# ScalarE copies both halves of an accumulator to a row, and VectorE adds the halves from that row

## The chip, the cores and the metric

The kernel runs on one core of a Trainium2 chip. The metric is the device time of one execution in microseconds (us), as the median of several runs. A profile is the hardware profiler's record of one further execution.

Five engines appear. PE is TensorE, and its record is split into matmuls (PE) and weight loads (PEld). DVE is VectorE, ACT is ScalarE, POOL is GpSimd, and SP is SyncE, which issues most of the DMAs. Each engine works through its own queue in order, and semaphores tie the queues together.

## The reference

One block of a hybrid network, on one sequence of 256 tokens with a model width of 2048, all in float32:

```python
z = h @ w_in                       # h: normalized x; all projections of the mixer at once
(dq, dkk, dv, dz, db, da, gq, gk, gv, glow, gr, su, gates) = split_columns(z, IN_SIZES)
qkv = silu(causal_depthwise_conv(concatenate([dq, dkk, dv]), dn_conv_w))
...                                # gated delta rule (DeltaNet), gated with silu(dz)
...                                # gated linear attention (GLA) from gq, gk, gv, glow, gr
...                                # S5 state space model over su, a scan over the 256 tokens
...                                # gates mix the three, then w_mix_out
...                                # cross-attention over 256 memory rows
...                                # FFN: two projections, a causal convolution over 3 tokens,
...                                # gelu of the one times the other, then the output projection
```

Widths of the projections: dq, dk, dv and dz 1024 each, gq and gk 512, gv, gr and su 1024, gates 3 x 2048; the FFN has 5632 hidden units, twice.

## The kernel before, in words

Every large matrix product is made in three partial products, so that the fast float32r format of TensorE gives nearly float32. The weights come by DMA as `raw` (SyncE, L205), 128 x 1024 at a time, which is two k-tiles of 128 rows by 512 columns. ScalarE casts them to their high part `whi` (L206) and VectorE subtracts to get the low part `wlo` (L206 too, since both stand in one line). There are four buffers of raw and three each of the high and the low part. The activations are held as a high and a low half beside each other, 2 x 256 columns.

`mm3` (L209 to L221) multiplies one 128 x 128 block: the high part of the weights with both halves at once, 512 columns, into all of an accumulator (L218, or L221 for the last k-tile), and the low part with the high half, 256 columns, into the first half of the accumulator (L219). So one accumulator is a PSUM bank of 128 x 512 whose two halves have to be added in the end. There are five such banks for accumulators ("acc") and three for other work ("mx").

`total` (L223) does that addition, and it is the function that changes. `proj` (L229) goes through one slab of 512 output columns: four accumulators, eight groups of weights for 16 k-tiles, and in the end the slab's `evac` for each of the four accumulators in turn. The evac functions call `total` and go on with the sum:

- `su_evac` (L1085, for the S5 input): total, then a product with `rx`, the inverse norm (L1090). rx comes out of work that waits for the whole of x (L992, L996).
- `conv_silu` (L382, for dq, dk and dv): total, an activation that scales it (L387), three steps of the convolution on VectorE (L389), Tanh (L392), a product (L393).
- the gated evac of dz and gr (L627 ff.), and those of keys and queries (L1183, L1184, L1335, L1343), some of which give `out`, the place for the sum.
- the FFN's evac (L1441 to L1458): total, a product with the inverse norm (L1444), and for every other accumulator the convolution (L1448, L1450) and the gelu (L1452); then the product of both (L1456) and its split in two parts (L305, L306).

152 totals are made in the program. `row()` gives a row of 128 x 256 from the pool `t1`, `row2()` one of 128 x 512 from the same pool; the evacuation of the gates (L1154) and the GLA's low-rank input use `row2` already.

The order of the instructions on each engine is not written out by hand: a scheduler with a model of the machine's times sets it when the program is built. `load_w` (L203) runs with a raised priority. Besides the projections there are background generators, which are fed in at set rates between the groups of weights: the set-up and the 255 steps of the S5 scan (VectorE, L932 to L934), the core of DeltaNet (L519, L702 to L722) and that of GLA. A change in what stands in a pool or an engine thus moves instructions elsewhere too.

Of the kernel before, what the change touches and what calls it, by code (L numbers as in the profile page):

```python
# [9 lines left out]
F32 = mybir.dt.float32  # L10
# [8 lines left out]
P = 128  # L19
T = 256  # L20
# [3 lines left out]
NW = 512  # L24
# [64 lines left out]
class Net:  # L89
# [131 lines left out]
            nc.tensor.matmul(acc, hi, both, start=start, stop=True)  # L221

    def total(self, acc, out=None):  # L223
        r = self.row() if out is None else out
        self.nc.scalar.copy(r, acc[:, T:2 * T])  # L225
        self.nc.vector.tensor_add(r, r, acc[:, 0:T])  # L226
        return r

    def proj(self, w, KT, rhs, evac, n=NW, wide=True):  # L229
# [81 lines left out]
    def open_main(self):  # L311
        c = self.ctx
        self.main_stack = ExitStack()
        self.sp = self.main_stack.enter_context(self.pool("sp"))
        self.s16 = self.main_stack.enter_context(self.pool("s16", bufs=1))
        self.s8 = self.main_stack.enter_context(self.pool("s8", bufs=3))
        self.s4 = self.main_stack.enter_context(self.pool("s4", bufs=6))
        self.t1 = self.main_stack.enter_context(self.pool("t1", bufs=8))
        self.jv = self.sp.tile([P, P], F32, name="jv")
        self.ja = self.sp.tile([P, T], F32, name="ja")  # L320

# [10 lines left out]
        return self.t1.tile([P, T], F32, name="r1", tag="r1")  # L332

    def row2(self):
        return self.t1.tile([P, NW], F32, name="r2", tag="r2", bufs=2)

    def small_cols(self, small, ab_in):
        nc = self.nc
# [1235 lines left out]
```

## Time and profile before

| what | value |
|---|---|
| runs shown | 1943.83, 1946.19 and 1947.27 us |
| their median | 1946.19 us |
| the profiled execution's own time | 1940.68 us |
| its span | 1938.9 us |
| mean granted clock of TensorE in it | 0.993 |
| bytes moved by DMA | 363.93 MB, 188 GB/s in the mean |

The span goes from the first to the last instruction of the profile; the time of the execution lies 1.8 us around it. In the rows below, a group's row reads: line of the code, engine, operation, output and inputs by their names in the program, form, count, then its busy time in us, the mean of one instruction in ns, and the idle time of the engine ahead of it with what ended that. A row of waits reads: engine and tile that waited, the arrow, the engine, tile and line waited for, then us in all, how often, and the longest. A row of a timeline starts with the instruction's start and its duration, and the bracket at its end is the idle time ahead of it and what ended it. A row of a stretch gives its bounds, its length and the busy time of PE, PEld, DVE, ACT and POOL, then the granted clock as a share of full speed, the DMAs' busy share and GB/s.

### The profile page before, as it was taken

The page shows a single profiled execution, that of the slowest core. Times are in us where ns is not written, and L with a number is a line of the kernel's source. Part 1 is how long each engine was busy: PE and PEld are TensorE (multiplying, and loading weights), DVE is VectorE, ACT ScalarE, POOL GpSimd, SP SyncE. Part 2 cuts the span into 40 slices and gives each one's busy share as a digit, 9 for nine tenths or more (in the row PEclk, how much of TensorE's full clock was granted, in tenths as well). Part 3 has the DMA queues.
Part 4 walks back from the last instruction along what each step waited for, and adds up shares of the span by engine and source line. Part 5 has one row for each costly group of instructions (what it writes and reads, how often), then busy time and mean ns, then how long its engine had stood idle before and what let it go on. Part 6 is the DMA issues. An engine that isn't in the chain of part 4 may idle for free.

```text
span 1938.9 us, 28177 instructions
## 1 busy us (share of the span) xinstructions
PE 1878.7 (97%) x10440; PEld 1565.4 (81%) x10440; DVE 1419.8 (73%) x2719; ACT 951.8 (49%) x1426; POOL 67.4 (3%) x117
## 2 busy tenths in 40 slices
PE   7989899999999999999999997999999999999997
PEld 6778788777778688878877986888888888888886
DVE  6878999996579999967666756766666666644445
ACT  5655544343565444444455655555555555534442
POOL 0000012020000000000000000000000000000000
PEclk9999999999999999999999998999999999999999
DMA  7535477684445576666576544655666555676664
GB/s 254 174 109 172 152 206 233 191 254 131 131 121 172 184 219 179 213 218 203 186 264 210 173 155 144 213 184 174 190 195 189 187 185 185 206 224 200 200 192 135
DMA packets 107482, 363.93 MB, mean 188 GB/s; under 512 B 12320, under 2 KB 20896, under 8 KB 106832
## 3 DMA queue, kind: packets, MB, share of 16 engines
q1 hardware_dynamic: 97696, 328.32, 54.9%
q0 software_dynamic: 9648, 33.81, 5.3%
q8 instruction: 82, 1.34, 0.3%
q14 instruction: 56, 0.46, 0.1%
HBM read 350.47 MB, written 11.61 MB: 187 GB/s over the span
## 4 chain that ended last, share of the span: by engine, by line
PE 86%; DVE 6%; issue 4%; DMA 2%; ACT 1%; POOL 0%; SPq 0%; DVEq 0%; ACTq 0%; POOLq 0%
PE acc L218 25%; PE acc L219 14%; PE acc L287 13%; PE acc L285 13%; PE acc L286 13%; DVE wlo L206 2%; PE acc L221 2%; PE mx L922 2%; DMA raw<-in 1%; DVE f L519 1%; DVE mm L932 0%; PE mx L183 0%; PE mx L947 0%; PE mx L641 0%; ACT whi L206 0%
## 5 line engine op out<-in xcount | busy, mean ns | idle before, releaser
L206 DVE TENSOR_TENSOR wlo<-raw,whi 128x1024 fp32r<-128x1024 f32 (+1 forms) x632 | 753.0, 1195 | 417.2 <-ACT whi L206 415.1
L206 ACT CAST whi<-raw 128x1024 fp32r<-128x1024 f32 (+1 forms) x632 | 646.7, 1029 | 724.8 <-PE acc L286 376.0
L218 PE MATMUL acc<-aa,whi 128*128 128x512 f32 x2085 | 725.8, 401 | 11.5 <-DVE r L226 9.7
L219 PE MATMUL acc<-aa,wlo 128*128 128x256 f32 x2224 | 555.2, 284 | 9.9 <-DVE wlo L206 9.9
L219 PEld LDWEIGHTS acc<-aa,wlo 128*128 128x128 f32 x2224 | 421.9, 190 | 53.3 <-DVE wlo L206 20.9
L218 PEld LDWEIGHTS acc<-aa,whi 128*128 128x128 f32 x2085 | 386.1, 190 | 82.2 <-issue 11.7
L285 PE MATMUL acc<-whi,aa 128*128 128x512 f32 (+1 forms) x704 | 269.8, 384 | 0.0
L286 PE MATMUL acc<-whi,aa 128*128 128x512 f32 (+1 forms) x704 | 268.4, 382 | 0.0
L287 PE MATMUL acc<-wlo,aa 128*128 128x512 f32 (+1 forms) x704 | 253.3, 385 | 3.7 <-DVE wlo L206 3.7
L287 PEld LDWEIGHTS acc<-wlo,aa 128*128 128x128 f32 x704 | 131.9, 188 | 33.6 <-DVE wlo L206 7.3
L286 PEld LDWEIGHTS acc<-whi,aa 128*128 128x128 f32 x704 | 132.4, 188 | 26.4 <-issue 1.1
L285 PEld LDWEIGHTS acc<-whi,aa 128*128 128x128 f32 x704 | 132.3, 188 | 26.2 <-issue 1.2
L285 PE MATMUL acc<-whi,ach 128*128 128x512 f32 x352 | 136.9, 389 | 0.0
L286 PE MATMUL acc<-whi,acl 128*128 128x512 f32 x352 | 136.9, 389 | 0.0
L287 PE MATMUL acc<-wlo,ach 128*128 128x512 f32 x352 | 123.4, 389 | 0.0
L932 DVE TENSOR_TENSOR mm<-M,X 128x128 f32<-128x128 f32 x254 | 98.6, 388 | 5.3 <-ACT X L926 0.6
L286 PEld LDWEIGHTS acc<-whi,acl 128*128 128x128 f32 x352 | 66.0, 188 | 13.8
L287 PEld LDWEIGHTS acc<-wlo,ach 128*128 128x128 f32 x352 | 66.1, 188 | 13.7
L285 PEld LDWEIGHTS acc<-whi,ach 128*128 128x128 f32 x352 | 66.1, 188 | 13.7
L934 DVE TENSOR_TENSOR X<-X,s__868 128x64 f32<-128x64 f32 x255 | 71.5, 280 | 4.5
L933 DVE TENSOR_TENSOR s__868<-mm 128x64 f32<-128x64 f32 x255 | 56.5, 222 | 4.7
L226 DVE TENSOR_TENSOR r<-r,acc 128x256 f32<-128x256 f32 x143 | 57.1, 414 | 0.4 <-ACT r L225 0.3
(454 smaller groups left out, 1865.6 us busy)
## 6 DMA issues: line engine op xcount, KB each, us to landing
raw<-in SPq DMA_DIRECT2D x600, 512.0 KB, 4.1
raw<-in SPq DMA_DIRECT2D x32, 256.0 KB, 2.7
gd<-r POOLq DMA_DIRECT2D x24, 256.0 KB, 4.7
f<-gd POOLq DMA_DIRECT2D x12, 512.0 KB, 5.3
f<-Rd POOLq DMA_DIRECT2D x4, 512.0 KB, 7.0
f<-in POOLq DMA_DIRECT2D x4, 512.0 KB, 4.0
gp<-in POOLq DMA_DIRECT2D x8, 256.0 KB, 4.5
xn<-in POOLq DMA_DIRECT2D x1, 2048.0 KB, 11.1
```

The costliest lines, as they stand in the source:

```text
L206: self.last = (nc.scalar.copy(hi, raw), self.seq(lambda: nc.vector.tensor_sub(lo, raw, hi.bitcast(F32))))
L218: nc.tensor.matmul(acc, hi, both, start=start, stop=False)
L219: nc.tensor.matmul(acc[:, :T], lo, x[:, 0, :], start=False, stop=False)
L221: nc.tensor.matmul(acc, hi, both, start=start, stop=True)
L226: self.nc.vector.tensor_add(r, r, acc[:, 0:T])
L285: nc.tensor.matmul(accs[t], xh[:, ts_], hi[:, kk, :], start=(kt == 0), stop=False)
L286: nc.tensor.matmul(accs[t], xl[:, ts_], hi[:, kk, :], start=False, stop=False)
L287: last[:] = [nc.tensor.matmul(accs[t], xh[:, ts_], lo[:, kk, :], start=False, stop=(kt == KT - 1))]
L922: nc.tensor.matmul(ps[:, n, c, :], self.Bl[c][rs, ft, :], su[rs, ft, tk], start=True, stop=True, tile_position=(32 * q, 0))
L932: nc.vector.tensor_mul(m, self.M, prev[:, None].broadcast_to([P, 2, 2, 32]))
L933: nc.vector.tensor_add(s, m[:, :, 0, :], m[:, :, 1, :])
L934: nc.vector.tensor_add(X[:, :, :, t], X[:, :, :, t], s)
```

## The change

`total` copies the whole accumulator, both halves, into a row of 128 x 512 from `row2`; VectorE then adds the two halves of that row, into its first half or into `out`. The pool `t1` loses two of its eight rows of 128 x 256, and the ring of `row2` has three rows instead of two. A sum without `out` lives in its row of the ring until its last reader is done.

```diff
     def total(self, acc, out=None):
-        r = self.row() if out is None else out
-        self.nc.scalar.copy(r, acc[:, T:2 * T])
-        self.nc.vector.tensor_add(r, r, acc[:, 0:T])
+        both = self.row2()
+        self.nc.scalar.copy(both, acc)
+        r = both[:, :T] if out is None else out
+        self.nc.vector.tensor_add(r, both[:, :T], both[:, T:])
         return r
...
-        self.t1 = self.main_stack.enter_context(self.pool("t1", bufs=8))
+        self.t1 = self.main_stack.enter_context(self.pool("t1", bufs=6))
...
     def row2(self):
-        return self.t1.tile([P, NW], F32, name="r2", tag="r2", bufs=2)
+        return self.t1.tile([P, NW], F32, name="r2", tag="r2", bufs=3)
```

Line numbers behind L225 are one higher after the change; the copy is L225 in both, the add L226 before and L227 after. The orders that follow were read from the built programs; a row is a line, an operation, and output and inputs, with a number on a tile's name where it tells one from another.

The first place is ScalarE's queue at the end of the dk projection, where `r_1054` and the like are the sums of the accumulators. Before:

```order
L206 CAST whi<-raw 128x1024 x3
L225 COPY r_1054<-acc 128x256
L206 CAST whi<-raw 128x1024
L387 ACTIVATE r_1057<-r_1054,cwh 128x256
L392 ACT_TABLE_LOAD
L392 ACTIVATE r_1062<-r_1057 128x256
L225 COPY r_1065<-acc 128x256
L387 ACTIVATE r_1068<-r_1065,cwh 128x256
L392 ACTIVATE r_1073<-r_1068 128x256
L225 COPY r_1086<-acc 128x256
L387 ACTIVATE r_1089<-r_1086,cwh 128x256
L206 CAST whi<-raw 128x1024 x5
```

After:

```order
L455 ACT_TABLE_LOAD
L455 ACTIVATE eg<-eg 128x16
L206 CAST whi<-raw 128x1024 x5
L225 COPY r_1054<-acc 128x512
L225 COPY r_1065<-acc 128x512
L225 COPY r_1086<-acc 128x512
L206 CAST whi<-raw 128x1024
L388 ACTIVATE r_1057<-r_1054,cwh 128x256
L206 CAST whi<-raw 128x1024
L393 ACTIVATE r_1062<-r_1057 128x256
L388 ACTIVATE r_1068<-r_1065,cwh 128x256
L225 COPY r_1097<-acc 128x512
```

Three copies now stand in a row, with five casts ahead of them, and the scalings (L387, now L388) and the Tanh (L392, now L393) stand behind; before, each copy stood behind the scaling of the accumulator ahead of it.

The second place is VectorE's queue at the same end of dk; `f_829` and `bl_450` belong to the set-up of the S5 scan, and `L893` (L894 after) is the first that reads what a DMA brings for it. Before:

```order
L206 TENSOR_TENSOR wlo<-raw,whi 128x1024
L389 SCALAR_TENSOR_TENSOR r_1057<-r_1054,cwh,r_1057 128x255
L389 SCALAR_TENSOR_TENSOR r_1057<-r_1054,cwh,r_1057 128x254
L389 SCALAR_TENSOR_TENSOR r_1057<-r_1054,cwh,r_1057 128x253
L393 SCALAR_TENSOR_TENSOR f_837<-r_1062,r_1057 128x4x64
L226 TENSOR_TENSOR r_1065<-r_1065,acc 128x256
L389 SCALAR_TENSOR_TENSOR r_1068<-r_1065,cwh,r_1068 128x255
L389 SCALAR_TENSOR_TENSOR r_1068<-r_1065,cwh,r_1068 128x254
L389 SCALAR_TENSOR_TENSOR r_1068<-r_1065,cwh,r_1068 128x253
L393 SCALAR_TENSOR_TENSOR f_837<-r_1073,r_1068 128x4x64
L226 TENSOR_TENSOR r_1086<-r_1086,acc 128x256
L893 TENSOR_TENSOR f_829<-f_824,bl_450 128x1024
```

After:

```order
L227 TENSOR_TENSOR r_1054<-r_1054 128x256
L227 TENSOR_TENSOR r_1065<-r_1065 128x256
L227 TENSOR_TENSOR r_1086<-r_1086 128x256
L206 TENSOR_TENSOR wlo<-raw,whi 128x1024
L390 SCALAR_TENSOR_TENSOR r_1057<-r_1054,cwh,r_1057 128x255
L390 SCALAR_TENSOR_TENSOR r_1057<-r_1054,cwh,r_1057 128x254
L390 SCALAR_TENSOR_TENSOR r_1057<-r_1054,cwh,r_1057 128x253
L206 TENSOR_TENSOR wlo<-raw,whi 128x1024
L394 SCALAR_TENSOR_TENSOR f_837<-r_1062,r_1057 128x4x64
L390 SCALAR_TENSOR_TENSOR r_1068<-r_1065,cwh,r_1068 128x255
L227 TENSOR_TENSOR r_1097<-r_1097 128x256
L894 TENSOR_TENSOR f_829<-f_824,bl_450 128x1024
```

The three adds now stand together and ahead of the convolution, and two subtractions of the weights (L206) stand between them and L894, where before the convolutions of two accumulators stood ahead of L893 and the next subtraction behind it.

The third place is ScalarE's queue at the end of su; `r_368` to `r_380` are the four sums, `rxr` the row of the inverse norm, `aa` the normalized activations. Before:

```order
L206 CAST whi<-raw 128x1024 x3
L225 COPY r_368<-acc 128x256
L225 COPY r_372<-acc 128x256
L225 COPY r_376<-acc 128x256
L206 CAST whi<-raw 128x1024
L225 COPY r_380<-acc 128x256
L206 CAST whi<-raw 128x1024 x2
L996 COPY rxr<-mx 128x256
L206 CAST whi<-raw 128x1024
L308 ACTIVATE aa<-f_102,vec 128x256 x4
```

After:

```order
L206 CAST whi<-raw 128x1024 x3
L225 COPY r_368<-acc 128x512
L225 COPY r_372<-acc 128x512
L225 COPY r_376<-acc 128x512
L206 CAST whi<-raw 128x1024
L997 COPY rxr<-mx 128x256
L225 COPY r_380<-acc 128x512
L309 ACTIVATE aa<-f_102,vec 128x256
L206 CAST whi<-raw 128x1024
L309 ACTIVATE aa<-f_102,vec 128x256
```

The fourth copy, which stood ahead of the copy of `rxr`, now stands behind it, and the casts that stood ahead of `rxr` stand behind both.

## The prediction

> **What bounds the kernel now.** I read the busy shares and the chain that ended last first, then the waits of TensorE (PE) over the whole span and by stretch.
>
> ```profile
> PE 1878.7 (97%) x10440; PEld 1565.4 (81%) x10440; DVE 1419.8 (73%) x2719; ACT 951.8 (49%) x1426; POOL 67.4 (3%) x117
> PE 86%; DVE 6%; issue 4%; DMA 2%; ACT 1%; POOL 0%; SPq 0%; DVEq 0%; ACTq 0%; POOLq 0%
> PE acc L219 <- DVE wlo L206: 10.6, 7, 4.3
> PE acc L218 <- DVE xset L1061: 9.7, 1, 9.7
> PE acc L218 <- DVE r L226: 9.7, 8, 2.2
> PE acc L218 <- DVE s__868 L933: 1.2, 1, 1.2
> ```
>
> PE is busy 97% of the span and carries 86% of the chain. A change that touches only VectorE (DVE) and ScalarE (ACT) can win no more than what PE waits for them. The third column of a wait is its longest, the first the total, the second the count. `DVE r L226` is the add of the two halves: eight times, 9.7 us in all, a matmul that starts a new accumulator waits until that add has read the old one and its bank is free. That is the sum the change can touch directly. ACT is half idle, so it has room for longer copies.
>
> Where these waits lie (the same view by stretch: 0 to 110, 110 to 240, 480 to 640 us):
>
> ```profile
> PE acc L218 <- DVE r L226: 3.3, 2, 2.2
> ...
> PE acc L218 <- DVE r L226: 4.4, 5, 1.6
> PE mx L398 <- DVE f L393: 2.1, 1, 2.1
> ...
> PE acc L218 <- DVE r L226: 2.0, 1, 2.0
> ```
>
> The rows of L226 add up to the 9.7. All lie at ends of projections whose evacuation has work ahead of the add in DVE's queue (the convolutions of DeltaNet at L389, the core of DeltaNet at L702). None lies in the convolutional FFN behind 1240 us, where most totals are.
>
> **What one total costs, before and after.**
>
> ```profile
> L225 ACT COPY r<-acc 128x256 f32<-128x256 f32 x143 | 49.4, 361 | 8.7 <-PE acc L221 8.6
> L226 DVE TENSOR_TENSOR r<-r,acc 128x256 f32<-128x256 f32 x143 | 57.1, 414 | 0.4 <-ACT r L225 0.3
> L1155 ACT ACTIVATE r<-acc 128x512 f32<-128x512 f32 x24 | 14.2, 593 | 9.9 <-PE acc L287 9.9
> L926 ACT COPY X<-mx 128x512 f32<-128x512 f32 x32 | 18.5, 585 | 8.9 <-PE mx L922 8.8
> L1444 DVE TENSOR_TENSOR r<-r,rfr 128x256 f32<-128x256 f32 x88 | 35.1, 420 | 0.7
> ```
>
> The copy of 128x256 takes 361 ns. A copy of 128x512 out of a PSUM bank stands in the trace twice, 585 and 593 ns, so each copy gets 0.23 us longer: over the 152 totals of the program (143 of them in these two rows) 35 us of ACT. ACT has 987 us (1938.9 − 951.8) without work, and it is off the chain but for 1%; I cost it at nothing except at the two places named below. The add loses its PSUM operand. L1444 is an element-wise product of the same shape out of rows in SBUF and takes 420 ns against 414: no gain and no loss on DVE. By the Trainium skill ("VectorE: DVE Perf Modes", "Rules for kernel authors") one should accept the slower PSUM operand, or copy to SBUF first only when many operations follow. One operation follows here, so by that rule the extra copy is not worth its price; its argument is the speed of the operation, and the two rows show no difference in that, so it moves no term.
>
> **Term A, the freed banks.** In the new order the copy alone frees the bank, and the add no longer does. At the end of dk, for example, ACT's three copies stand in a row right behind five casts, and the convolution's activations (L387, L392) come after them; before, each copy stood behind the activations of the row before.
>
> ```profile
> 573.56 0.37 ACT L225 COPY r<-acc 128x256 f32<-128x256 f32 x1 [2.67 <-PE acc L221]
> 578.11 0.43 DVE L226 TENSOR_TENSOR r<-r,acc 128x256 f32<-128x256 f32 x1
> 578.59 0.50 PE L218 MATMUL acc<-aa,whi 128*128 128x512 f32 x1 [2.02 <-DVE r L226]
> 583.98 0.47 PE L218 MATMUL acc<-aa,whi 128*128 128x512 f32 x1 [1.23 <-DVE s__868 L933]
> ```
>
> The copy was over at 573.93, and the add came at 578.11, behind the DeltaNet core's own work in DVE's queue; the matmul that wanted the bank waited 2.02 us for it. A copy of 0.59 us is over before the next projection has taken the spare bank, so the whole wait goes. I count the last row as one of the same kind under another name: it is the start of the next accumulator after 578.59, and the add that frees its bank stands in DVE's queue right ahead of the L933 named. So A is −9.7 − 1.2 = −10.9. The other end: in the stretch to 110 us PE may then wait for the next weights instead (term C shows that DVE is late there), and the 3.3 are not won: −7.6. I take −10.9.
>
> **Term B, the half clock behind a wait.** The granted clock of single stretches (last columns: PEclk, DMA share, GB/s; the first after the bounds is PE's busy time):
>
> ```profile
> 221.30:224.70 3.40, 0.75 (x6) 0.47 (x5) 3.40 (x15) 0.81 (x3) 0.00 (x0) 1.00 0.00 0
> 224.70:228.10 3.40, 3.40 (x11) 2.92 (x12) 3.40 (x9) 2.17 (x3) 0.00 (x0) 0.51 0.00 0
> 576.30:579.70 3.40, 1.38 (x8) 0.97 (x7) 3.40 (x8) 2.49 (x4) 0.00 (x0) 1.00 0.60 210
> 579.70:583.10 3.40, 3.06 (x11) 2.32 (x9) 3.40 (x7) 0.62 (x2) 0.00 (x0) 0.50 0.45 131
> ```
>
> Behind a stretch in which PE worked 1.38 of 3.40 us, the next 3.4 us run at half the clock; that costs half of them, 1.7. The one at 579.7 comes from the wait at 577 alone; the one at 224.7 has 2.1 us of another wait in it too (the transposes at L398). So −1.7 to −3.4; I take −2.5. The Trainium skill ("TensorE: Matmul & The Clock Gate", "What's actually happening") has the clock fall only after a whole idle window of about 3.4 us. The trace differs: 2.0 us of waiting were enough at 577. By the page B would be 0, which is the third rival below.
>
> **Term C, a DMA at the end of dk.**
>
> ```profile
> 102.81 1.23 DVE L893 TENSOR_TENSOR f<-f,bl 128x1024 f32<-128x1024 f32 x1 [2.67 <-DMA f<-zd]
> 107.90 0.39 PE L219 MATMUL acc<-aa,wlo 128*128 128x256 f32 x1 [4.35 <-DVE wlo L206]
> 108.70:112.10 3.40, 3.40 (x12) 2.86 (x11) 3.40 (x5) 1.04 (x1) 0.00 (x0) 0.50 0.86 264
> ```
>
> DVE stands 2.67 us at L893 for the DMA that brings the coefficients of the S5 scan, and the low half of the next weights stands behind it: PE starves 4.35 us and runs at half the clock after that (1.7). In the new order two more of these subtractions of L206 stand ahead of L893 (L894 in the new numbering), so the wait of DVE falls beside PE's work. Gain up to −6.0; at the other end 0, if DVE is merely late by as much elsewhere. I take −4.0, since two weights ahead feed PE for 11.5 us (32 matmuls for each, of 0.18 us by the page's 1878.7 over 10440), longer than DVE waits.
>
> **Term D, a new wait on rows of the ring.** The sums now live in a ring of three rows of 128x512. At the end of su the fourth copy needs the row of the first sum, which is released by L1090, and that waits for rx (the copy at 46.88).
>
> ```profile
> 45.48 1.23 DVE L206 TENSOR_TENSOR wlo<-raw,whi 128x1024 fp32r<-128x1024 f32 x1 [1.05 <-ACT whi L206]
> 46.88 0.36 ACT L996 COPY rxr<-mx 128x256 f32<-128x256 f32 x1
> 49.93 2.76 DVE L1122 TENSOR_TENSOR f<-f,rxr 128x256 f32<-128x256 f32 x8
> 53.71 1.21 DVE L206 TENSOR_TENSOR wlo<-raw,whi 128x1024 fp32r<-128x1024 f32 x1
> ```
>
> Queued behind that copy on ACT is the cast of the next weights, which DVE's L206 waits for, which PE waits for. In the new order the subtraction that ran at 45.48 comes after the products of L1122, where the one of 53.71 stands now, so it would end near 55 instead of 46.7. When PE reaches it no row tells; with one weight in stock (5.8 us, as in C) it would be at about 51 to 52, and PE would stand for 3 to 6 us with what follows. DVE is busy 41.9 of the 45 us from 40 to 85, so some of it is regained while it catches up. At the lower end 0 (the wait falls into the idle of ACT ahead of it), at the upper +6. I take +4.0.
>
> **Term E, the slabs of the FFN.** The wait of the weight load for `wlo` recurs once in each of the 20 slabs:
>
> ```profile
> 1331.03 0.42 ACT L1452 ACTIVATE r<-r 128x256 f32<-128x256 f32 x1 [0.77 <-DVE r L1450]
> 1331.60 2.00 ACT L206 CAST whi<-raw 128x1024 fp32r<-128x1024 f32 x2
> 1333.96 0.19 PEld L219 LDWEIGHTS acc<-aa,wlo 128*128 128x128 f32 x1 [0.41 <-DVE wlo L206]
> PEld acc L219 <- DVE wlo L206: 7.4, 19, 0.4
> ```
>
> ACT's next casts stood behind the gelu (L1452) of the second row; now a cast stands before each gelu, with the copies ahead. PE itself has no row of waits in this stretch, since the loads run ahead of their matmuls, so of the 7.4 I count at most half, −3.7, and at least 0. I take −1.5, a fifth.
>
> **What costs nothing.** One more load of an activation table (at dk's end there are two where one was) falls into ACT's idle. The steps of the S5 scan on DVE shift by some ten against the weights after dk and are level again some 80 weights later, where DVE has idle time. No DMA is issued in another order by SyncE; GpSimd has one swap of neighbours.
>
> **Sum.** −10.9 − 2.5 − 4.0 + 4.0 − 1.5 = −14.9. Against the profiled execution's own 1940.68 that is 1925.8. It lies 5.5 under the median of the runs, so I forecast 1946.2 − 14.9 = 1931.3. With the good ends −10.9 − 3.4 − 6.0 + 0 − 3.7 = −24.0 (1922.2), with the bad ones −7.6 − 1.7 − 0 + 6.0 − 0 = −3.3 (1942.9).
>
> **Rivals.**
>
> 1. DVE is the bound from 40 to 270 us, and the waits only change their name.
>
> ```profile
> 40.00:85.00 45.00, 42.98 (x256) 36.43 (x254) 41.92 (x150) 27.04 (x46) 1.08 (x2) 1.00 0.56 176
> 85.00:240.00 155.00, 140.96 (x839) 120.56 (x838) 128.69 (x318) 79.69 (x127) 3.20 (x5) 0.98 0.48 147
> 240.00:270.00 30.00, 30.00 (x142) 24.91 (x141) 29.41 (x69) 16.62 (x25) 1.15 (x2) 1.00 0.67 199
> ```
>
> DVE's busy time is the third after the bounds: 41.92 of 45, 128.69 of 155, 29.41 of 30. The change takes no work off it. If its idle stays, the 3.3 + 4.4 come back as waits for `wlo`, C and the clock at 224.7 stay, and only 2.0 + 1.2 + 1.7 at 577 and 584 and D remain: −0.9, so 1945.3. Against it speak the 26 us that DVE idles from 85 to 240.
>
> 2. Slower: the ring of three rows holds ACT at every projection. A fourth copy needs the row whose last reader is the convolution's or gate's last product; ACT, which runs in order, stands with the casts behind it. At 0.77 us, the idle of ACT ahead of the gelu in the row above, 38 projections (152 totals by four) would cost 29.3: −14.9 + 29.3 = +14.4, so 1960.6. It decides from 0.5 us for each (19 us against −14.9). Against it: ACT has half its time free, and in the FFN's new order two casts stand between the third and the fourth copy.
>
> 3. The half clock doesn't hang on these waits (its stretches begin at fixed times), and B is nothing: −12.4, so 1933.8.
>
> **The numbers.** My sum: 0.60. Rival 1: 0.16. Rival 2: 0.14. Rival 3: 0.10. What differs by under 0.2% (3.9 us: 1942.3 to 1950.1) cannot be told from no change by this measurement. My sum and rival 3 lie below, 0.70 faster; rival 1 is no change, 0.16; rival 2 slower, 0.14. The range goes from 1922, the good ends, to 1948, which takes in rival 1 with the runs' own scatter (up to 1947.3) and leaves out rival 2. The likeliest case's own is 1922.2 to 1943.
>
> **What the profile after would show.** The name of the add vanishes from PE's waits, and no wait for the copy takes its place by more than 1 us in all (A). The clock is whole from 579 to 583 and from 224 to 228 (B). `wlo` waits below 1 us near 105 (C). A new wait for `wlo` of 3 to 6 us near 52, with ACT's copy in front of it waiting for DVE (D). PEld's waits for `wlo` behind 1240 shrink from 7.4 (E). Copies at 0.59 and adds at 0.41 to 0.42 us. I am wrong if the copies wait at many projections for a row, if DVE's idle from 85 to 240 stays at 26 us, or if D is not one place but several.

## The result, and the profile after

The changed kernel takes 1931.6 us in the median of four runs (1928.4 to 1934.36) against 1945.9 (1943.83 to 1947.27): ratio 0.9929, 95% interval 0.9918 to 0.9941. That is 14.3 us less; 14.9 were forecast. A second comparison gave 1935.1 against 1946.6, ratio 0.9946 (0.9930 to 0.9963), or 11.5 us. The two agree within their intervals.

The profiled execution took 1932.46 us with a span of 1930.7, clock 0.991. The page's busy times and its chain:

```profile
PE 1876.0 (97%) x10440; PEld 1571.3 (81%) x10440; DVE 1418.2 (73%) x2719; ACT 985.2 (51%) x1427; POOL 67.4 (3%) x117
PE 72%; DVE 1%; issue 1%; ACT 0%; DMA 0%; DVEq 0%; POOL 0%; ACTq 0%; POOLq 0%
```

ACT works 33.4 us more, near the 35 costed; DVE and PE do the same work within 3 us. PE still has by far the largest share of the chain. What PE waits for after the change, over the whole span:

```profile
PE acc L219 <- DVE wlo L206: 12.7, 5, 4.6
PE acc L218 <- DVE xset L1062: 10.3, 1, 10.3
PE acc L288 <- DVE wlo L206: 4.3, 10, 1.4
PE mx L923 <- DVE rsot L194: 2.2, 1, 2.2
PE acc L218 <- ACT r L225: 0.8, 1, 0.8
```

The row `DVE r L226`, 9.7 us at eight places, has no successor: no matmul that starts an accumulator waits for the add any more, and one waits 0.8 us for the copy. But `wlo` costs more than before (12.7 against 10.6), in fewer and longer waits, and `rsot` is new. Copies and adds, by form:

```profile
L225 ACT COPY r<-acc 128x512 f32<-128x512 f32 x151 | 86.5, 581 | 8.7 <-PE acc L221 4.6 <-DVE f L1091 0.5 <-DVE f L1162 0.3
L227 DVE TENSOR_TENSOR r<-r 128x256 f32<-128x256 f32 x144 | 55.9, 418 | 2.5 <-ACT r L225 2.3
```

A copy takes 581 ns, an add out of SBUF 418 against 414 out of the bank: the sizes forecast. ACT's copies waited for a row of the ring for 0.8 us in the whole program (the two releasers on DVE).

Around the two places where the clock had halved, PE is now busy without a gap and the clock stays at 1.00 (the third number from the end):

```profile
216.00:226.00 10.00, 10.00 (x59) 8.73 (x59) 9.87 (x28) 5.73 (x9) 0.00 (x0) 1.00 0.58 178
573.00:583.00 10.00, 10.00 (x72) 8.70 (x67) 10.00 (x18) 7.62 (x12) 0.00 (x0) 1.00 0.45 132
```

What got worse stands at three places. First the end of su (timeline after; ACT, then DVE, then PE):

```profile
47.03 0.37 ACT L997 COPY rxr<-mx 128x256 f32<-128x256 f32 x1 [8.06 <-PE mx L995]
47.90 0.58 ACT L225 COPY r<-acc 128x512 f32<-128x512 f32 x1 [0.49 <-DVE f L1091]
49.74 1.04 ACT L206 CAST whi<-raw 128x1024 fp32r<-128x1024 f32 x1
54.73 1.21 DVE L206 TENSOR_TENSOR wlo<-raw,whi 128x1024 fp32r<-128x1024 f32 x1
48.54 0.50 PE L218 MATMUL acc<-xset,whi 128*128 128x512 f32 x1 [0.84 <-ACT r L225]
55.99 0.58 PE L219 MATMUL acc<-xset,wlo 128*128 128x256 f32 x1 [3.42 <-DVE wlo L206]
```

ACT stands 8.06 us at the copy of the norm; behind it stands the fourth copy of su, whose row comes free only with L1091, which needs that norm, and behind that the casts, two of which before ran ahead of it at 44.40 and 45.93. DVE's next subtraction comes at 54.73, and PE stands 0.84 and 3.42 us. Second, the end of dk: the store of the S5 coefficients and the loads that bring them back (GpSimd issues both), with their first reader. Before:

```profile
91.81 0.55 POOL L883 DMA_DIRECT2D zd<-zs  x1 [48.36 <-DVE zs L881]
94.81 2.65 POOL L887 DMA_DIRECT2D f<-zd  x4 [2.46 <-DMA zd<-zs]
```

After:

```profile
92.36 0.55 POOL L884 DMA_DIRECT2D zd<-zs  x1 [48.57 <-DVE zs L882]
98.29 2.65 POOL L888 DMA_DIRECT2D f<-zd  x4 [5.38 <-DMA zd<-zs]
99.55 1.22 DVE L206 TENSOR_TENSOR wlo<-raw,whi 128x1024 fp32r<-128x1024 f32 x1 [1.30 <-ACT whi L206]
107.26 1.23 DVE L894 TENSOR_TENSOR f<-f,bl 128x1024 f32<-128x1024 f32 x1 [5.42 <-DMA f<-zd]
111.21 0.58 PE L219 MATMUL acc<-aa,wlo 128*128 128x256 f32 x1 [4.64 <-DVE wlo L206]
```

The store was issued 0.55 us later, but GpSimd, which issues the loads behind it, stood 5.38 us for its completion instead of 2.46, and the reader starts at 107.26 instead of 102.81. What moved beside it, in the stretch behind the store, before and after (PE's busy time first, GB/s last):

```profile
94.00:96.00 2.00, 0.71 (x5) 0.39 (x3) 0.18 (x2) 1.75 (x3) 1.19 (x2) 1.00 0.64 234
```

```profile
94.00:96.00 2.00, 2.00 (x14) 1.73 (x13) 1.31 (x4) 1.85 (x3) 0.00 (x0) 1.00 0.93 314
```

Third, the end of gk, where ACT's wide copies stand ahead of DVE's adds and these ahead of the products (L954) that free a bank of PE's. Before, PE's longest wait there was this one:

```profile
485.08 1.15 PE L922 MATMUL mx<-f,bl 32*128 32x128 f32 x8 [1.24 <-ACT f L605]
```

After:

```profile
477.31 1.09 ACT L225 COPY r<-acc 128x512 f32<-128x512 f32 x2
477.94 0.92 DVE L227 TENSOR_TENSOR f<-r 128x256 f32<-128x256 f32 x2 [0.55 <-ACT r L225]
479.50 0.43 DVE L227 TENSOR_TENSOR f<-r 128x256 f32<-128x256 f32 x1 [0.65 <-ACT r L225]
482.64 2.04 PE L923 MATMUL mx<-f,bl 32*128 32x128 f32 x8 [2.18 <-DVE rsot L194]
```

The balance of the two traces follows from PE's gaps: the distances between the starts of consecutive matmuls, each less a fixed length for its columns, 213 ns for 512, the same in both traces (undisturbed, the matmuls of 512 columns follow each other at 224 to 233 ns). For the clock it follows from the runs of matmuls at twice their usual distance:

| term | forecast | in the traces |
|---|---|---|
| A: waits for the add (94, 99, 168, 194, 218, 576 and 582 us) | −10.9 | −11.4 |
| the wait of the transposes at 221 and the one behind it | none | −3.0 |
| B: half clock at 225 and 580 | −2.5 | −2.7 |
| C: wait for `wlo` at the end of dk, with its half clock | −4.0 | +1.2 |
| D: stop at su, with half clock (1.2) | +4.0 | +5.0 |
| E: slabs of the FFN | −1.5 | −4.0 |
| waits at 464 to 490 us, with half clock (1.7) | 0 | +4.8 |
| other (a wait at 66 gone, 1.2; small gaps) | 0 | +1.9 |
| sum | −14.9 | −8.2 |

The two profiled executions differ by 8.2 us, the runs by 14.3. The profiled execution of before was faster than all its timed runs, so the traces hold less of the gain than the medians do.

### The profile page after: what moved, and what is told of

Its sections match the earlier page's. It is cut to its first block, busy times and chain, and to the rows that moved or that the text cites. A ratio compares the mean times of both kernels' runs of the same rounds, so it can differ in the third digit from the quotient of the medians.

```text
span 1930.7 us, 28100 instructions
## 1 busy us (share of the span) xinstructions
PE 1876.0 (97%) x10440; PEld 1571.3 (81%) x10440; DVE 1418.2 (73%) x2719; ACT 985.2 (51%) x1427; POOL 67.4 (3%) x117
## 4 chain that ended last, share of the span: by engine, by line
PE 72%; DVE 1%; issue 1%; ACT 0%; DMA 0%; DVEq 0%; POOL 0%; ACTq 0%; POOLq 0%
PE acc L218 20%; PE acc L286 12%; PE acc L288 12%; PE acc L287 12%; PE acc L219 11%; PE acc L221 1%; PE mx L923 1%; PE mx L642 0%; PE mx L183 0%; PE mx L720 0%; DMA mch<-in 0%; DVE wlo L206 0%; PE mx L755 0%; DVE aa L1479 0%; PE mx L948 0%
## 5 line engine op out<-in xcount | busy, mean ns | idle before, releaser
L206 DVE TENSOR_TENSOR wlo<-raw,whi 128x1024 fp32r<-128x1024 f32 (+1 forms) x632 | 754.6, 1195 | 422.9 <-ACT whi L206 420.5
L206 ACT CAST whi<-raw 128x1024 fp32r<-128x1024 f32 (+1 forms) x632 | 650.2, 1030 | 775.8 <-PE acc L287 388.0
L218 PE MATMUL acc<-aa,whi 128*128 128x512 f32 x2085 | 717.9, 399 | 0.6 <-DVE aa L1298 0.4
L219 PE MATMUL acc<-aa,wlo 128*128 128x256 f32 x2224 | 545.8, 283 | 9.3 <-DVE wlo L206 9.3
L219 PEld LDWEIGHTS acc<-aa,wlo 128*128 128x128 f32 x2224 | 421.3, 190 | 49.5 <-DVE wlo L206 12.2
L218 PEld LDWEIGHTS acc<-aa,whi 128*128 128x128 f32 x2085 | 382.2, 189 | 65.0 <-issue 1.4
L287 PEld LDWEIGHTS acc<-whi,aa 128*128 128x128 f32 x704 | 133.0, 189 | 26.3 <-issue 0.7
L225 ACT COPY r<-acc 128x512 f32<-128x512 f32 x151 | 86.5, 581 | 8.7 <-PE acc L221 4.6
```

The lines of the kernel that those rows point to most:

```text
L206: self.last = (nc.scalar.copy(hi, raw), self.seq(lambda: nc.vector.tensor_sub(lo, raw, hi.bitcast(F32))))
L218: nc.tensor.matmul(acc, hi, both, start=start, stop=False)
L219: nc.tensor.matmul(acc[:, :T], lo, x[:, 0, :], start=False, stop=False)
L225: self.nc.scalar.copy(both, acc)
L287: nc.tensor.matmul(accs[t], xl[:, ts_], hi[:, kk, :], start=False, stop=False)
```

## The experiments

Times are medians of 4 to 11 runs; differences are taken before rounding. The kernels were timed in three groups, each on another chip and beside the kernel before. The first group is the changed kernel again, the bank held by the add, su's sums in place and the FFN alone (before: 1946.6 us). The second is the kernel before again, the ring apart with and without the stop at su, and the coefficients without their way through memory (1946.1). The third is the ring of two rows, the held bank without the stop at su, the wide copy for dz and gr, and the four rows (1946.7). Times of different groups are set side by side as they are, since the three times of before lie within 0.6 us.

**The kernels themselves again.** No edit. First the changed kernel:

> The changed kernel once more, with more rounds, since the traces so far differ by 8.2 us (1938.9 to 1930.7) and the medians by 14.3. If the gain is what the traces show (waits for banks gone, new ones at su and near 480 us), the ratio comes out between 0.992 and 0.996. If the first comparison was a good draw, it lies at 0.995 or above; if the first profile of before was the odd one, at 0.9925 again.

Measured: 1935.1 us, ratio 0.9946 (0.9930 to 0.9963). Then the kernel before:

> The kernel before, unchanged, for the scatter of profile and runs: ratio 0.998 to 1.002. Its first profile ran 1940.7 us, below all its timed runs but few; if that one was a good draw, this one runs 1943 to 1948 us with the same waits for the add (9.7 us at eight places) and a few us more elsewhere.

Measured: 1946.5 us, ratio 0.9999 (0.9990 to 1.0008). Its profiled execution took 1943.1 us, again below the median of its runs, by 3.4 us; those of the changed kernel took 1932.5 and 1933.0. So the first trace of before was a good draw by 2.4 us, and by the mean of two traces each the change is 9.2 us. What makes the timed runs of before longer than its profiled ones stays open.

**The bank held by the add.**

```diff
-        self.nc.vector.tensor_add(r, both[:, :T], both[:, T:])
+        self.nc.vector.tensor_add(r, both[:, T:], acc[:, :T])
```

> The copy of both halves and the ring stay, but VectorE adds the first half from the bank, so that the add frees the bank as it did before; ScalarE's price and the rows are those of the changed kernel. Theory (the freed banks make the gain): PE's waits for the add come back, 8 us or more, with half clock behind one or two; ratio to before 0.998 to 1.006, some 12 us above the changed kernel. Rival (another order and other pools make the gain): it stays within 3 us of the changed kernel, ratio 0.992 to 0.995.

Measured: 1939.8 us, ratio 0.9964 (0.9951 to 0.9977). PE's waits for the add:

```profile
PE acc L218 <- DVE r L227: 3.8, 3, 2.0
```

Both theories miss. Of the eight places with 9.7 us one comes back, at 584 us with 2.0; two more, at 434 and 438 us with 1.5 and 0.3, are places where the kernel before had no such wait. Those at the ends of dk and dq, 94 to 225 us, do not come back, although the add frees the bank there as it did before. So something else had removed them.

**A ring of their own for the sums.** The old total, and nothing else than the rows changed:

```diff
-        r = self.row() if out is None else out
+        r = self.row3() if out is None else out
...
-        self.t1 = self.main_stack.enter_context(self.pool("t1", bufs=8))
+        self.t1 = self.main_stack.enter_context(self.pool("t1", bufs=5))
...
+    def row3(self):
+        return self.t1.tile([P, T], F32, name="r3", tag="r3", bufs=3)
```

> The total of before (ScalarE copies one half, VectorE adds the other from the bank), but the sums get a ring of their own, three rows of 128x256 beside five rows for the rest, in place of eight rows shared with the convolutions' own rows. With the bank held by the add and VectorE's price unchanged, the waits at the ends of dk and dq were gone already; theory: what ends those waits is that a sum no longer queues for a row behind the convolution of the sum before it, so the order at dk's end is three copies and three adds together here too, and the waits for the add at 94 to 218 us go, with the one at 577 staying and the stop at su coming in: ratio 0.994 to 0.999, near the kernel that holds the bank. Rival (the bank's early release makes the whole gain): 0.999 to 1.003.

Measured: 1928.3 us, ratio 0.9907 (0.9889 to 0.9924): 17.9 us faster than before, with the narrow copy and the add from the bank. That is more than both forecasts allowed; what would stay and what would come in was forecast rightly, the stop at su (3.4 us) too. Waits of PE from 85 to 640 us:

```profile
PE acc L219 <- DVE wlo L206: 4.7, 1, 4.7
...
PE acc L218 <- DVE r L226: 2.0, 1, 2.0
...
PE acc L285 <- DVE f L226: 0.5, 1, 0.5
```

Two waits for an add are left, 2.0 us at 572 and 0.5 at the end of gk. By PE's gaps the gain lies at the end of dq (18.3 us between 160 and 232 us before, 9.6 here) and in the FFN (43.8 and 39.0 from 1240 to 1700 us). From 40 to 160 us nothing is won (31.4 and 32.7): the stop at su and the wait for the S5 coefficients, both here too, take what the end of dk gives. ACT's order at the end of dk is the changed kernel's:

```order
L206 CAST whi<-raw 128x1024 x6
L225 COPY r_1054<-acc 128x256
L225 COPY r_1065<-acc 128x256
L225 COPY r_1086<-acc 128x256
L206 CAST whi<-raw 128x1024
L390 ACTIVATE r_1057<-r_1054,cwh 128x256
```

In the kernel before, the copy of each sum stood behind the Tanh of the sum before it, in just the sequence in which the program asks its one ring of eight rows for sum, scaled sum and Tanh. That this sequence is what tied the copies down is inferred from the orders; that a ring apart unties them and takes the waits away is measured. (Up to the GLA the rows have the same number of bytes as before. The cross-attention and the FFN take theirs from pools of their own, of 6 and 12 rows, and get the three rows on top.)

**The same ring with two rows** (`bufs=2`, and six for the rest).

> The old total with a ring of its own for the sums, of two rows instead of three (and six rows for the rest). In its order the third copy at dk's end stands behind the activations of the first sum again, and the coefficients' reader further back. Theory (the ring sets how many sums can leave their banks): waits for the add come back at the ends of dk and dq, some 3 to 6 of the 11 us, and the time lies between the kernel with three rows (1928.3) and before (1946.3): 1931 to 1942. Rival (any ring of its own does it): 1926 to 1931.

Measured: 1960.3 us, ratio 1.0069 (1.0054 to 1.0084), slower than before. In ACT's order the third copy at dk's end stands behind a Tanh again. But the waits of PE for the add come to 3.6 us in all, and 2.0 of them are the one near 590 that three rows leave too; so 1.6 came back, at 50 and 103 us, where 3 to 6 were forecast for the ends of dk and dq. From 40 to 130 us others stand beside them:

```profile
PE acc L219 <- DVE wlo L206: 5.5, 2, 4.7
PE mx L925 <- DVE bl L901: 3.1, 1, 3.1
PE acc L218 <- DVE r L226: 1.6, 2, 0.9
PE acc L218 <- DVE small L1118: 1.6, 1, 1.6
```

Behind them PE has half the clock for 17 us on end, its busy time the first and the clock the third from the end:

```profile
110.00:127.00 17.00, 16.57 (x68) 14.16 (x68) 11.95 (x28) 9.61 (x18) 0.00 (x0) 0.50 0.21 62
```

Up to 1900 us the stretches at half clock come to 44.4 us, with three rows to 20.5; at half the work lost in each, that is up to 12 of the 32 us. The weight loads' waits for `wlo` in the FFN are back as well, with 8.9 us. The size of the ring decides over more than the whole change does; that the kernel would fall behind the one before was not foreseen.

**The stop at su.** The changed kernel, with the sums of su in their own place:

```diff
-        nc.vector.tensor_mul(n.su[:, m, :], n.total(acc), rx[0])
+        nc.vector.tensor_mul(n.su[:, m, :], n.total(acc, n.su[:, m, :]), rx[0])
```

> The changed kernel, but at su the add writes its sum into the place of the S5 input, and the product with the inverse norm is made in place there, so the ring's row is free after the add and the fourth copy need not wait for the norm. Theory (the ring holds ScalarE at su): the stop of 0.8 + 3.4 us near 50 us and the half clock behind it go, 5 us. The order of VectorE near 106 us changes with it: five subtractions of weights instead of three between the store of the S5 coefficients and their first reader, so the wait for that DMA (4.6 us and 2.6 of half clock) may go as well. Time 5 to 12 us below the changed kernel, ratio to before 0.987 to 0.991. Rival (VectorE's work sets the pace up to 110 us anyway, and a stop saved at 50 comes back as a wait later): within 2 us of the changed kernel.

Measured: 1921.2 us, ratio 0.9873 (0.9861 to 0.9886), 14.0 us below the changed kernel in the same group and the fastest of all that ran. What is left of the waits of PE:

```profile
PE acc L218 <- DVE xset L1062: 10.3, 1, 10.3
PE acc L219 <- DVE wlo L206: 8.2, 6, 2.4
```

The wait of 3.4 us at su is gone, and in place of the one of 4.6 at dk stand 1.6 and 1.4 us, at 117 and 122 us. No stretch at half clock is left between 20 and 500 us. Time and places were forecast. In the traces the gain is 12.3 us (1930.7 and 1918.4): 7.5 of it by PE's gaps from 40 to 160 us, less than the 5.0 + 7.4 that the trace after gives for the two places, 1.2 from 420 to 500 us, where no half clock follows the waits any more, and the rest in small pieces.

**The S5 coefficients without their way through memory** (their four loads left out, GpSimd fills the tile):

```diff
-        for q in range(4):
-            self.side.dma_start(out=zt[32 * q:32 * q + 32].rearrange("p c f s -> p (c f) s"),
-                                in_=zd[q:64:4, :][None].broadcast_to([32, 16, P]))
+        self.side.memset(zt.rearrange("p c f s -> p (c f s)"), 0.01)
```

> The changed kernel with the four loads that bring the S5 coefficients back from memory left out (GpSimd fills that tile with a constant, so the S5 part of the output is another). Theory (VectorE stands at L894 for a DMA that shares the queues with the weights): PE's wait of 4.6 us near 106 us and the half clock behind it (2.6) go; 3 to 8 us below the changed kernel. Rival (VectorE is late there by its own work): within 2 us of the changed kernel, the wait stays.

Measured: 1922.5 us, ratio 0.9881 (0.9863 to 0.9898), 9.2 us below the changed kernel's first median and 12.7 below its second. PE has no wait for `wlo` above 0.5 us between 85 and 130 us; the stop at su (3.4) is still there. The forecast, 3 to 8 us, was too small. In the traces the gain is 8.8 us, and 7.2 of it lie in PE's gaps from 40 to 160 us, where the trace after shows 4.8 of waiting and 2.6 of half clock. So DVE's stop at L894 cost about that; the rest came with an order that had changed elsewhere too (the store is issued at 105.93 us here).

**The change in the FFN alone.** Everywhere else the old total and pools.

> The change in the FFN's totals alone (from 1240 us on); everywhere else the old total and the old pools. Theory (each slab of the FFN wins some 0.2 us, since its casts come before the gelu): the trace gains 4 us behind 1240 us and nothing before, ratio 0.997 to 0.999. Rival (the FFN's 4 us hang on what happened earlier): no change, 0.999 to 1.001.

Measured: 1941.8 us, ratio 0.9980 (0.9972 to 0.9989): 4.8 us, as the theory had it. A sum of PE's gaps by 50 us drops from 4.8 to 4.4 in every slice of the FFN, here as in the changed kernel, and to 4.3 with the ring of three rows alone. So this term does not need the wide copies; rows apart, three more than before in this pool, give it too.

**The early release and the wide copy, without the stop at su.** Both edits were made with su's sums in place: the add from the bank with both halves copied, and the old total with the ring of three rows.

> Both halves copied, su's sums in their own place, but the add reads the first half from the bank and frees it. Beside 1921.2 (the copy frees the bank) it prices the early release alone. Theory: the wait of 2.0 us near 565 and one or two more for the add come back with half clock: 1925 to 1932. Rival (the release is worth nothing once the sums have a ring): 1919 to 1923.

Measured: 1930.0 us, ratio 0.9914 (0.9899 to 0.9928).

```profile
PE mx L923 <- DVE rsot L195: 2.4, 1, 2.4
PE acc L218 <- DVE r L227: 2.4, 2, 2.0
```

The forecast holds in the time and in the waits for the add, but no half clock follows them; it follows the wait for `rsot`.

> The same, with the sums of su added into their own place as well, so that neither the ring nor ScalarE stops at su. Theory (the ring's gain, less the stop at su): 5 to 12 us below the kernel with the ring alone. Against the kernel with both halves copied and su's sums in place (1921.2) it lacks the release of banks by the copy: 3 to 8 us above it, 1924 to 1930. Rival (the copy of both halves is what matters): 10 us or more above it.

Measured: 1925.0 us, ratio 0.9891 (0.9876 to 0.9905). That is 3.2 us below the ring alone, where 5 to 12 were forecast, and 3.8 above 1921.2, as forecast. Side by side:

| | stop at su | su's sums in place |
|---|---|---|
| ring apart, narrow copy, add frees the bank | 1928.3 | 1925.0 |
| wide copy, add frees the bank | 1939.8 | 1930.0 |
| wide copy, copy frees the bank (the change) | 1935.1 | 1921.2 |

The release by the copy is worth 4.7 us in the one column (the intervals of the two ratios overlap) and 8.9 in the other. PE's waits for the add are only 3.8 and 2.4 of that; the rest comes with the order. The wide copy by itself costs 11.6 and 5.0. (The ring of the wide rows is also that of the gates, and the rest has six rows instead of five, so this price holds more than the copies' length.) Together they give +6.9 (+3.3 with the changed kernel's first median) and −3.8.

**The wide copy only where a bank waits** (dz and gr; the ring apart and su's sums in place elsewhere):

```diff
-        nc.scalar.activation(c, self.total(acc), AF.Copy, scale=0.5)
+        nc.scalar.activation(c, self.total_wide(acc), AF.Copy, scale=0.5)
```

> The old total in a ring of its own, su's sums in place, and the copy of both halves only in the gated evacuations (dz and gr), where a wait for the add is left. Theory: the 2.0 us near 565 and the half clock behind it go, 1920 to 1924 beside 1925.0 without it. Rival (dz's wider copies and the two rows of their ring cost what the bank gives): 1924 to 1930.

Measured: 1923.9 us, ratio 0.9885 (0.9869 to 0.9902). The wait of 2.0 is gone, with one of 1.1 for `wlo` in its place, and the wait for `wlo` near 106 us has grown from 2.4 to 3.6 us with another order. So the gain is 1.1 us and lies within the scatter.

**Four rows in the ring of the wide sums** (and four for the rest; su's sums in place):

> The kernel with both halves copied and su's sums in place, with four rows for the sums and four for the rest instead of three and six: all four copies of a projection can go in a row. Theory (the ring was the limit): the fourth copy comes earlier at every projection, a gain of 0 to 4 us on 1921.2. Rival (four rows for the convolutions' own are too few): slower by 2 to 8 us.

Measured: 1924.7 us, ratio 0.9894 (0.9876 to 0.9911), 3.5 us above the kernel with three rows, as the rival had it, though the intervals of the two ratios overlap. The wait at the end of dk is back with 4.0 us. A fourth row won nothing.

## Why the prediction was right, step by step, and where not

The time came out at 1931.6 against 1931.3. That the two agree to 0.3 us is luck: three terms were right, two were off by 5 us in the wrong direction, one fell short, 3.0 us at the transposes were not forecast, and the traces show 8.2 to 10.1 us where the runs show 11.5 to 14.3.

- **A** was right in size and places (−11.4 for −10.9) and wrong in its cause. The prediction said that the copy alone now frees the bank, and so the wait goes. With the bank still held by the add, seven of the eight places were quiet, in the kernel with the ring apart as in the one with the wide copy. Only the wait at 577, where DVE is deep in DeltaNet's core, needs the release. The rest went because the sums have rows of their own. The prediction showed that order ("three copies in a row") and ascribed its effect to the copy.
- **B** was right: −2.7 for −2.5. The stretches at half clock went with the waits, and new ones came behind new gaps, at 55, 110 and 482 us, so the third rival falls. One part of it holds: in every trace the stretches begin whole multiples of 3.413 us apart (before at 108.68, 224.74 and 579.72 us, 34 and 104 multiples apart). So it counts how a wait falls on this grid. The one of 2.02 us at 577 left PE busy for 41% of a stretch of the grid, and half the clock followed; the one of 2.18 us at 95 left it 45%, and none followed. In three of the other traces half the clock also follows stretches full of matmuls on 32 rows (L923 or L925), so PE's busy time alone does not decide. The rule of a whole idle window, which the prediction cites from the Trainium skill ("TensorE: Matmul & The Clock Gate", "What's actually happening"), is too narrow for the row at 577, as the prediction said; at su, where a wait of 3.42 us stands ahead, the trace does not speak against it.
- **C** was the step that failed: "two weights ahead feed PE for 11.5 us", with 32 matmuls for each, so that DVE's wait would fall beside PE's work. Each weight has 16 matmuls (four accumulators, two k-tiles, two products), so two feed PE for 5.8 us: DVE's last subtraction ahead of L894 ended at 100.77, and PE stopped at 106.57. Nor is DVE's wait all that lies between two subtractions; its own work there is 3.7 us, and a subtraction takes 1.2. Even with the 2.67 us of waiting that were counted this makes 7.6 us, more than 5.8, so the wait would have reached PE. The wait itself grew too, since the DMA came 4.4 us later. PE ran without its stops from 92 to 106 us, the DMAs moved 228 to 314 GB/s in the stretches from 92 to 98 us where they had moved 152 to 234, and the small store beside them took 5.38 us to complete. The other traces fit: from the issue of the store to the landing of the last load pass 10.5 to 11.0 us in the three traces in which PE still has its stops there (before, twice, and the FFN alone), and 12.2 to 16.3 in the ten others with the loads in them (14.9 after). That the traffic is what holds them up is inferred. The Trainium skill ("DMA: Bandwidth & Descriptors", "Latency and other measured facts") says that the fixed cost of a transfer grows with the load on the memory; the two completions, 2.46 and 5.38 us, agree in direction.
- **D** was right in place, chain and size (+5.0 for +4.0), as the kernel with su's sums in place confirms. Its place (52.6 us for 51 to 52) came out in part by luck, since the 5.8 us for one weight in stock are 2.9 by the count under C. The second rival, which had the same stop at every projection, does not hold: ACT waited 0.8 us for rows in the whole program. The kernel with two rows came to 1960.3, near that rival's 1960.6, but not on its way: ACT's copies waited 1.5 us for rows there.
- **E** was mis-sized: −4.0, where −1.5 was taken of at most −3.7. All of the gaps went, not a part: the wait of the weight load for `wlo` in the FFN, 7.4 us before, has no row after.
- **"ACT costs nothing"** fell. The cover that was named, ACT's idle half, does not help where DVE waits for the copy: at the end of gk the chain of copies, adds and products reaches PE, +4.8 with its half clock. PE's gaps from 420 to 500 us are 18.0 to 23.0 us in all seven traces with the wide copy at gk, and 14.3 to 15.7 in the six with the narrow one and rows enough (21.9 with the ring of two rows). Beside the same release of the bank, the wide copy with its rows costs 5.0 to 11.6 us.
- **The first rival** (DVE sets the pace to 270 us and the waits change their name) holds in part. From 40 to 160 us PE's gaps did not shrink (31.4 us before, 32.7 after): what the end of dk gave went to su and to the DMA. From 160 to 232 us the gain stayed (18.3 and 9.6). DVE's idle time from 85 to 240 us, which the prediction named as a sign against itself, fell only from 26.3 to 23.5.

## What to carry to other kernels

Before a wait for a bank is put down to the instruction that frees it, look at which ring the evacuation takes its rows from: the order here was set by a ring that sums and scratch rows shared, and a ring of three rows apart won more (17.9 us) than the change did. A result that is kept until a late operand comes should not sit in a short ring, since whoever needs its row next stops with all that is queued behind: writing it to its final place was worth 14.0 us in the changed kernel, 9.8 with the bank held and 3.2 with the ring apart. And when a wait of the leading engine goes, ask which transfers it will now start earlier, and what small round trip through memory runs beside them.

## What the runs showed that was not expected

A store of 32 KB to memory took 2.46 us to complete at a moment with 152 to 234 GB/s of traffic and 5.38 at one with 228 to 314. Over all fourteen traces the same store took 1.9 to 3.7 us beside a mean of 171 to 254 GB/s, and 4.0, 4.8 and 5.3 us beside 267, 310 and 289. So the longest stand beside the most traffic, but traffic does not tell the rest: 2.0 and 3.4 us both stand beside 216. And a ring of two rows instead of three for sums of 128x256 moved this kernel by 32 us, 1960.3 against 1928.3, with nearly the same busy time on DVE (1423 and 1418 us) and ACT (954 and 957).
